# A 90-degree rotation on one core: all loads and stores on one SP queue in a fixed order, in place of loads on SP and stores on ACT

## The chip, the cores and the metric

The kernel runs on one core of one Trainium2 chip. The metric is device time in microseconds (us), the median of repeated executions. The profile's span, from the first to the last instruction, is about 1.8 us shorter than that time. With one core there is no second die to compare with.

## The reference

```python
def setup_inputs():
    batch, c, h, w = 32, 3, 256, 256
    return {"x": np.random.randn(batch, c, h, w).astype(np.float32)}

def reference(x):
    return np.rot90(x, k=-1, axes=(-2, -1)).astype(np.float32)
```

96 images of 256 x 256 fp32 are turned by 90 degrees. 25.17 MB are read and 25.17 MB written; there is no arithmetic.

## The kernel before

The images are cut into 24 slabs of 1 MB. Each of the 128 partitions holds 8 whole rows (8 KB, contiguous in memory on both sides). VectorE turns a slab with two transposes; it reads one tile and writes another, so loads, transposes and stores of different slabs can overlap.

```python
    in_pool = ctx.enter_context(tc.tile_pool(name="in_pool", bufs=12))
    out_pool = ctx.enter_context(tc.tile_pool(name="out_pool", bufs=12))

    for n in range(n_slabs):                                  # 24 slabs
        t_in = in_pool.tile([P, R * W], fp32, tag="t_in")
        nc.sync.dma_start(out=t_in, in_=ld_v[n])              # load: SP queue

        t_out = out_pool.tile([P, R * W], fp32, tag="t_out")
        src = t_in.rearrange("p (r g c) -> p c r g", r=R, c=R)
        dst = t_out.rearrange("p (c g r) -> p c r g", c=R, r=R)[:, :, ::-1, ::-1]
        for k in range(PARTS):                                # 2 transposes
            cs = slice(k * CP, (k + 1) * CP)
            nc.vector.transpose(out=dst[:, cs], in_=src[:, cs])

        nc.scalar.dma_start(out=st_v[n], in_=t_out)           # store: ACT queue
# ... (shapes, views and launch cut)
```

## Time and profile before

| | before |
|---|---|
| median time | 124.7 us |
| span of the profiled execution | 122.9 us |
| bytes moved | 50.34 MB |
| VectorE busy | 94.6 us (77%) |
| loads, stores: issue to landing, median | 19.6 us, 16.5 us |

First the page of the profile before. The rows with 40 figures cut the span into 40 equal slices of 3.07 us: busy tenths for an engine or for the 16 DMA engines (9 is 90% or more), then the rate in GB/s. q1 is the SP queue, q10 the ACT queue, q14 the one that the page calls instruction; the last column is the share of the 16 engines' time.

```profile
span 122.9 us, 186 instructions
...
DVE  0199999999897697796977967979769779797500
...
DMA  2999999999999999999999999999999999999994
GB/s 93 427 427 403 339 424 427 427 429 427 427 432 427 427 427 427 432 429 427 427 427 427 429 427 427 427 427 429 427 427 427 427 429 427 427 429 427 427 424 171
...
q1 hardware_dynamic: 3456, 25.17, 49.2%
q10 hardware_dynamic: 3456, 25.17, 48.5%
...
DMA 89%; DVE 2%; DVEq 2%; SPq 1%; issue 0%
```

The DMA engines are full in every slice but the first and last, the rate is near 427 GB/s, and 89% of the chain of waits is DMA. VectorE has gaps. This kernel is limited by data movement alone: 50.33 MB at 427 GB/s take 117.9 us of the span's 122.9. The rest is the start (the first packet starts at 1.80 us), the exit, and one dip. The dip is in slices 4 and 5 (403, 339), seen finer in the stretches of 1 us of before; the last two columns are the DMA share and GB/s:

```profile
10.00:11.00 1.00, 1.00 (x1) 0.00 (x0) 1.00 1.07 451
11.00:12.00 1.00, 1.00 (x2) 0.00 (x0) 1.00 0.94 360
12.00:13.00 1.00, 1.00 (x1) 0.00 (x0) 1.00 1.06 311
13.00:14.00 1.00, 1.00 (x2) 0.00 (x0) 1.00 0.96 287
14.00:15.00 1.00, 1.00 (x1) 0.00 (x0) 1.00 0.94 393
15.00:16.00 1.00, 1.00 (x2) 0.00 (x0) 1.00 0.99 418
```

Against 427, the four low rows lack 67 + 116 + 140 + 34 = 357 KB, which is 0.84 us at that rate, although the engines count as busy (share near 1). Here a DMA share near 1 stood beside 287 GB/s as well as beside 427, so read the share beside the rate. In the trace's packet records, the loads' 8 KB packets took 393 ns on average from 11 to 15 us, against 309 ns from 5 to 10 us. The first store had been issued at 9.67 us. The page also counts 768 packets under 512 B, 16 for each of the 48 transfers; in the packet records they have 4 bytes and took 9 ns each. The expectations below call them completion records.

One more view will matter: the way out, as the groups of the exit line of before (count; shortest, median and longest in ns; start of the first and of the last in us). SP's first DRAIN, at 122.16 us, comes after SP's last wait on a transfer, which ended at 122.12; POOL's semaphore steps run from 122.2 to 122.8 us, and the span ends at 122.9.

```profile
L79 POOLq EVENT_SEMAPHORE  x4: 17/17/17, 122.2 to 122.8; - x4
L79 SPq DRAIN  x3: 7/7/7, 122.2 to 122.5; - x3
```

### The profile page before, as it was taken

The numbers are of one execution on the slowest core, as the hardware profiler recorded it, in microseconds if no ns is written. First come the engines' busy times: TensorE is split into PE (matmuls) and PEld (weight loads), VectorE is DVE, ScalarE is ACT, GpSimd is POOL, SyncE is SP. The second block draws the span as 40 slices with busy tenths as digits, with TensorE's granted clock in tenths as the row PEclk, the third lists the DMA queues.
The fourth block names the chain that finished last, engine by engine and source line by source line (L and its number), as shares of the span: only waits on it lengthen the run. The fifth ranks groups of instructions, "written<-read, shape, count | busy, mean of one in ns | idle before, by whom it ended". The sixth has DMA issues, their size and how long they took to land.

```text
span 122.9 us, 186 instructions
## 1 busy us (share of the span) xinstructions
DVE 94.6 (77%) x48; POOL 0.2 (0%) x4
## 2 busy tenths in 40 slices
DVE  0199999999897697796977967979769779797500
POOL 0000000000000000000000000000000000000000
DMA  2999999999999999999999999999999999999994
GB/s 93 427 427 403 339 424 427 427 429 427 427 432 427 427 427 427 432 429 427 427 427 427 429 427 427 427 427 429 427 427 427 427 429 427 427 429 427 427 424 171
DMA packets 6913, 50.34 MB, mean 410 GB/s; under 512 B 768, under 2 KB 768, under 8 KB 768
## 3 DMA queue, kind: packets, MB, share of 16 engines
q1 hardware_dynamic: 3456, 25.17, 49.2%
q10 hardware_dynamic: 3456, 25.17, 48.5%
q14 instruction: 1, 0.01, 0.0%
HBM read 25.17 MB, written 25.17 MB: 410 GB/s over the span
## 4 chain that ended last, share of the span: by engine, by line
DMA 89%; DVE 2%; DVEq 2%; SPq 1%; issue 0%
DMA t_in<-in_x_dram 89%; DVE t_out L51 2%; DVEq L79 2%; SPq L44 1%; DVEq L51 0%
## 5 line engine op out<-in xcount | busy, mean ns | idle before, releaser
L51 DVE STREAM_TRANSPOSE t_out<-t_in 128x1024 f32<-128x1024 f32 x48 | 94.6, 2052 | 20.9 <-DMA t_in<-in_x_dram 15.4
L68 POOL MEMSET const-uint8-127<- 128x1 uint8 x1 | 0.1, 102 | 0.0
L68 POOL MEMSET const-bfloat16-1.0<- 128x1 bf16 x1 | 0.1, 101 | 0.0
L68 POOL MEMSET const-float32-0.0<- 128x1 f32 x1 | 0.1, 98 | 0.2 <-issue 0.2
L68 POOL MEMSET const-float32-1.0<- 128x1 f32 x1 | 0.1, 98 | 0.0
## 6 DMA issues: line engine op xcount, KB each, us to landing
t_in<-in_x_dram SPq DMA_DIRECT2D x24, 1024.0 KB, 19.6
out_dram<-t_out ACTq DMA_DIRECT2D x24, 1024.0 KB, 16.5
```

The costliest lines, as they stand in the source:

```text
L44: nc.sync.dma_start(out=t_in, in_=ld_v[n])
L51: nc.vector.transpose(out=dst[:, cs], in_=src[:, cs])
L68: nc = _bacc.Bacc("TRN2", target_bir_lowering=False, num_devices=1)
L79: with _tile.TileContext(nc) as tc:
```

## The change

The intent: let one queue carry all transfers in an order that the program fixes, so that loads stay a set distance of nine slabs ahead and each store takes its turn.

```diff
+    AHEAD = 9
+    ins = []
+
+    def load(n):
+        t_in = in_pool.tile([P, R * W], fp32, tag="t_in")
+        last = nc.sync.dma_start(out=t_in, in_=ld_v[n])
+        ins.append(t_in)
+        return last
+
+    for n in range(AHEAD):
+        load(n)
+
     for n in range(n_slabs):
-        t_in = in_pool.tile([P, R * W], fp32, tag="t_in")
-        nc.sync.dma_start(out=t_in, in_=ld_v[n])
         t_out = out_pool.tile([P, R * W], fp32, tag="t_out")
-        src = t_in.rearrange("p (r g c) -> p c r g", r=R, c=R)
+        src = ins[n].rearrange("p (r g c) -> p c r g", r=R, c=R)
         # ... transposes as before
-        nc.scalar.dma_start(out=st_v[n], in_=t_out)
+        nc.sync.dma_start(out=st_v[n], in_=t_out)
+        if n + AHEAD < n_slabs:
+            load(n + AHEAD)
```

Each transfer waits for the landing of the one eight places earlier in the order, because the compiled program has eight semaphores for transfers (99, 100 and 102 to 107 in both traces). Before, loads held four of the eight in steady state (99, 102, 104, 106) and stores the other four. If only the loop is rewritten, with stores left on ACT, the compiled order is the same as before (built and compared, not run): on two queues the rewritten loop is no change at all. The change therefore is the one queue. It takes SP from 24 transfers to 48.

## The prediction

> **What bounds the kernel now.** The 16 DMA engines. The page's slice rows show DMA at 9 (90% or more) in every slice but the first and last, with 427 GB/s in most. The kernel moves 50.33 MB; at 427 GB/s that is an estimated 117.9 us of the 122.9 us span. The stretch table shows where the other 5 us are: nothing moves before about 2 us; after 121.1 us there is only the last receipt and the exit (1.91 us at the end of the chain of waits); and from 11 to 15 us the rate is 360, 311, 287, 393 GB/s while the DMA engines stay busy, which lacks about 0.36 MB, or 0.84 us. This dip comes just as the first store, issued at 9.67 us, mixes with the loads. VectorE is no limit: two transposes take 3.98 us a slab, against 4.9 us for a load plus a store. [...]
>
> **What the change does.** It adds no bytes, transpose or transfer. 24 stores move from the ACT queue to SP, which then issues 48 transfers of about 0.33 us, one per 2.45 us of transfer: no limit. [...] the rate is 427 with loads alone (4 to 10 us), with both mixed, and with stores alone (after 112 us). A mixed single queue no trace shows yet.
>
> Will the fixed order starve the engines? In the compiled order each transfer waits for the one eight places before it, and each store for its transposes. Eight transfers are 19.6 us of work. Slab n's transposes end at about 9.5 + 3.9n us; its store's turn comes at about 2 + 2.45 x (9 + 2n) = 24 + 4.9n us. The slack is 14 us and grows. At the end nine stores go out in a row; the last load lands near 98 us, its transposes end near 103 us, and its store is not due before about 117 us. VectorE is not exposed at the tail.
>
> **On the critical path.** Only the 0.84 us dip can go, if the two queues cause it; if it is a cost of the first stores, it moves to about 24 us and stays. Half of it, 0.4 us, is my expected gain. Against it stands a risk: switching direction inside one queue may cost a gap. [...]
>
> **Predicted time: 124.3 us**, 8 in 10 between 123.3 and 126.2. Faster by over 2%: 0.04; within 2%: 0.87; slower by over 2%: 0.09.
>
> **What would show each step.** Right: one queue with near 98% of the engines' time, 427 GB/s from 3 to 120 us, no dip at 11 to 15 us; SP's waits all on transfers, never long on VectorE; VectorE's last work near 103 us, stores alone in the last 20 us; landing near 19.6 us for both kinds. Wrong: a mixed stretch (24 to 100 us) below 420 GB/s with DMA busy (a switching cost), or slices with DMA under 9 in the middle (starved: SP held by a wait).
>
> **What would make it wrong.** A queue too shallow for eight transfers, so that SP stalls; a switch cost; or a gain in the mixed stretch from runs in one direction, which loads alone, at 427, speak against.

## The result, and the profile after

| | before | after |
|---|---|---|
| median time | 124.72 us (124.66 to 124.83) | 125.12 us (125.09 to 125.14) |
| span of the profiled execution | 122.9 us | 123.3 us |
| VectorE's last transpose ends (timeline) | 115.4 us | 104.0 us |
| loads, stores: issue to landing, median | 19.6, 16.5 us | 19.6, 19.6 us |

The ratio is 1.0031, with a 95% interval of 1.0013 to 1.0048: the same within 2%, but a real 0.4 us slower. Ratios here are the mean time of one kernel's fast runs over that of the other's fast runs of the same rounds, so not quite the ratio of the medians. Executions over 1.5% slower than the fastest of the same kernel are left out of the means.

The page after:

```profile
span 123.3 us, 177 instructions
...
DVE  0199999999999999999999996796976977000000
...
DMA  3999999999999999999999999999999999999993
GB/s 93 422 428 428 425 425 422 353 388 428 428 425 428 425 428 428 428 425 428 428 425 428 428 425 430 433 425 425 428 428 428 425 428 428 428 422 428 430 425 130
...
q1 hardware_dynamic: 6912, 50.33, 97.7%
```

One queue now takes 97.7% of the engines' time, as both together did, and at the same rate. The stretch table gives 427 GB/s over 30 to 100 us in both kernels. VectorE works without gaps from 5.6 to 74.6 us, because loads are far ahead, and is done 19 us before the end; none of that made the run shorter (125.12 us against 124.72). The dip is in slices 8 and 9 now. After, by microsecond:

```profile
22.00:23.00 1.00, 1.00 (x2) 0.00 (x0) 1.00 1.05 434
23.00:24.00 1.00, 1.00 (x1) 0.00 (x0) 1.00 1.16 360
24.00:25.00 1.00, 1.00 (x2) 0.00 (x0) 1.00 1.04 246
25.00:26.00 1.00, 1.00 (x1) 0.00 (x0) 1.00 0.82 328
26.00:27.00 1.00, 1.00 (x2) 0.00 (x0) 1.00 0.98 418
```

It lacks 67 + 181 + 99 = 347 KB, or 0.81 us, against 0.84 before. It has moved to the time when the first store gets its turn behind nine loads (9 x 2.45 us after the first bytes), and has kept its size.

SP's own waits, after (what SP waited for; us in total, times, longest):

```profile
SPq L65 <- DMA out_dram<-t_out: 34.1, 16, 2.2
SPq L50 <- DMA t_in<-in_x_dram: 30.3, 16, 3.0
...
SPq L65 <- DVE t_out L63: 3.7, 4, 1.5
```

A store that waits for VectorE holds up every load behind it in the fixed order: ahead_2, below, waited so for 118.5 us and took 147.25 us. Here it happened four times, by 1.5 us at most, with up to 19.6 us of transfers queued ahead.

So where do the 0.4 us come from? Not from the transfers. The records of SP's last wait on a transfer start at 122.09 us before and 122.06 us after: by SP's waits, the changed kernel had all its data in place 0.04 us earlier. The difference comes after that. The exit line's groups, after:

```profile
L93 POOLq EVENT_SEMAPHORE  x4: 17/17/17, 122.7 to 123.2; - x4
...
L93 SPq DRAIN  x3: 7/7/130, 122.1 to 122.9; - x3
```

SP's first DRAIN comes at 122.1 (122.2 before), but POOL's answer to the second comes at 122.7 (122.2 before), and one DRAIN now takes 130 ns in place of 7. In the trace's records SP's first two DRAINs start at 122.160 and 122.215 before (0.06 us apart), and at 122.125 and 122.535 after (0.41 us apart). From SP's first DRAIN to POOL's answer it is 0.09 us before and 0.57 us after: 0.48 us more, less the 0.04 us gained, is the 0.44 us between the spans (122.89 and 123.33 in the records).

### The profile page after: what moved, and what is told of

It reads as the page before. It is cut to its first block, busy times and chain, and to the rows that moved or that the text cites. A ratio compares the mean times of both kernels' runs of the same rounds, so it can differ in the third digit from the quotient of the medians.

```text
span 123.3 us, 177 instructions
## 1 busy us (share of the span) xinstructions
DVE 92.9 (75%) x48; POOL 0.2 (0%) x4
## 3 DMA queue, kind: packets, MB, share of 16 engines
q1 hardware_dynamic: 6912, 50.33, 97.7%
## 4 chain that ended last, share of the span: by engine, by line
DMA 77%; SPq 2%; DVE 2%; DVEq 2%; issue 1%
DMA t_in<-in_x_dram 77%; SPq L50 2%; DVE t_out L63 2%; DVEq L93 2%
## 5 line engine op out<-in xcount | busy, mean ns | idle before, releaser
L63 DVE STREAM_TRANSPOSE t_out<-t_in 128x1024 f32<-128x1024 f32 x48 | 92.9, 2048 | 11.1 <-DMA t_in<-in_x_dram 5.6
## 6 DMA issues: line engine op xcount, KB each, us to landing
t_in<-in_x_dram SPq DMA_DIRECT2D x24, 1024.0 KB, 19.6
out_dram<-t_out SPq DMA_DIRECT2D x24, 1024.0 KB, 19.6
```

## The experiments

Two questions were open: what makes SP pause on its way out, and what the dip is. For the pause, theory A says that it belongs to the length of SP's instruction list; its rival B says that it belongs to the queue that issued the last stores. For the dip, theory F says that it comes once, with the first store; its rival M says that it comes with every turn from a stretch of loads to stores. All twelve kernels gave correct results. Diffs are against the changed kernel, unless it is said that they are against the one before.

### The last store back on ACT (last_store_act)

```diff
-        nc.sync.dma_start(out=st_v[n], in_=t_out)
+        q = nc.scalar if n == n_slabs - 1 else nc.sync
+        q.dma_start(out=st_v[n], in_=t_out)
```

> The changed kernel, with only the last of the 24 stores moved back to the ACT queue. The traces of before and after show the last store landed at the same time (SP's last wait ends 122.12 and 122.08 us), and then 0.55 us less or more on the way out: SP's second exit step follows its first by 0.06 us before, by 0.41 us after. Theory A (length): SP's instruction list is now twice as long[...]; one store less changes nothing, the gap stays near 0.4 us and the time near 125.1 us. Theory B (owner): the queue that issued the last store pays on its way out; with the last store on ACT the gap on SP goes to under 0.1 us and the time to about 124.7 us.

Measured: 124.96 us (124.87 to 124.98), ratio 1.0013 (1.0001 to 1.0025), between the two expectations. The exit groups tell why:

```profile
L94 POOLq EVENT_SEMAPHORE  x4: 17/17/17, 122.2 to 123.0; - x4
L94 SPq DRAIN  x3: 7/7/130, 122.1 to 122.7; - x3
```

The long DRAIN of 130 ns is still there, but POOL's first answer is back at 122.2: it is the third DRAIN now that comes late (122.745 us, 0.60 us after the second, against 0.24 us before). One transfer less takes two instructions out of SP's list (87 to 85), and the pause came two of SP's records later. Counted from the start of the trace, it is before SP's 80th record in both kernels. Part of it is now hidden: from SP's first DRAIN to the end of the span it is 1.00 us here, 1.21 in the changed kernel and 0.73 in the one before. This refutes the sharp form of B (the pause follows the last store) and suggests a fixed place in SP's list.

### Two slabs in one transfer (two_slabs)

```diff
-    AHEAD = 9
+    AHEAD = 4
+    S = 2                                   # tiles [P, S, R * W], 6 buffers each
-    ... .rearrange("(n p r) w -> n p (r w)", p=P, r=R)
+    ... .rearrange("(n s p r) w -> n p s (r w)", s=S, p=P, r=R)
 # ... stores likewise; transposes loop over s
```

> The changed kernel with two slabs (2 MB) in each transfer: one SP queue, four double loads ahead, 24 transfers in all in place of 48, all on SP. Theory A (length): SP has no more instructions than before, so the exit gap of 0.4 us is gone and the time is at most 124.7 us; with half the completion records (9 ns each, 24 fewer on each engine, 0.2 us) about 124.5 us. Theory B (owner): SP still issues the last store, the gap of 0.4 us stays, and the time is about 124.9 us. The dip at the first store should stay in both, near 23 us.

Measured: 125.28 to 127.15 us in the five fast executions (median 125.76), a wide scatter. The time misses both expectations. SP waited 12 times and 90.7 us in all for VectorE, since a double slab is ready only after four transposes, and the last data landed later (SP's first DRAIN at 122.7); that the waits caused this was not shown. The exit itself, with the last store on SP and a list of 49 instructions, has no pause: SP's DRAINs are 0.06 and 0.24 us apart, as before:

```profile
L95 SPq DRAIN  x3: 7/7/7, 122.7 to 123.0; - x3
```

That is A and not B. The dip was smaller here: 328 and 377 GB/s from 21 to 23 us lack 99 + 50 = 149 KB, or 0.35 us.

### Loads in halves of 64 partitions, stores on ACT (half_loads; against before)

```diff
-        nc.sync.dma_start(out=t_in, in_=ld_v[n])
+        for h in (slice(0, P // 2), slice(P // 2, P)):
+            nc.sync.dma_start(out=t_in[h], in_=ld_v[n][h])
```

> The kernel before with each load cut in two halves of 64 partitions: 48 loads on SP, 24 stores on ACT. SP's list is as long as in the changed kernel, but no store is on SP. Theory A (length): the exit gap on SP rises to about 0.4 us. Theory B (owner): it stays at 0.06 us. The time has 24 more completion records per engine, 9 ns each, 0.2 us: about 125.3 us under A, 124.9 us under B; the trace decides rather than the time.

Measured: 147.32 to 148.76 us in the three fast executions, wrong by about 23 us, and no pause. As a test of the pause it failed, because SP's list turned out to be 75 instructions (71 records) and not 87: it ends before the 80th record, so neither theory is touched. The time taught something else. Rates by slice, in half_loads:

```profile
DMA  5999999999999999999999999999999999999936
GB/s 115 215 215 215 213 374 363 416 379 379 226 292 385 401 385 326 365 279 397 403 423 281 379 399 385 401 383 365 405 392 350 401 383 379 421 321 370 419 159 250
```

While only half loads ran (slices 2 to 5) the rate was 215 GB/s, just half of 428, with the DMA engines busy all the time. The packet records say how: from 4 to 15 us an 8 KB packet took 605 ns on average, against 309 ns in the loads of before. Each packet took twice as long. The column cuts below ask whether the partitions or the size did it.

### A small store at the very start (warm_store)

```diff
+    warm_pool = ctx.enter_context(tc.tile_pool(name="warm_pool", bufs=1))
+    scratch = nc.dram_tensor("scratch", (P, 128), fp32, kind="Internal").ap()
+    t_w = warm_pool.tile([P, 128], fp32, tag="t_w")
+    nc.vector.memset(t_w, 0.0)
+    nc.scalar.dma_start(out=scratch, in_=t_w)
```

> The changed kernel with one extra store of 64 KB of zeros to a scratch tensor, on the ACT queue, issued at the very start. The dip (360, 246, 328 GB/s at 23 to 26 us in the changed kernel, 360, 311, 287, 393 at 11 to 15 us before) came with the first store in both. Theory F (first store, once per run): the dip moves to the first 5 us, none at 23 to 26 us; time between 124.3 (hidden in the start) and 125.2 us. Theory M (the turn from loads alone to a mix): the dip stays at 23 to 26 us, and the time stays at 125.1 us or 0.2 us more.

Measured: 125.12 us (125.11 to 125.28), as the changed kernel. The stretches around the dip:

```profile
23.00:24.00 1.00, 1.00 (x2) 0.00 (x0) 1.00 1.00 418
24.00:25.00 1.00, 1.00 (x2) 0.00 (x0) 1.00 1.08 336
25.00:26.00 1.00, 1.00 (x2) 0.00 (x0) 1.00 0.91 352
26.00:27.00 1.00, 1.00 (x2) 0.00 (x0) 1.00 0.97 410
```

The dip is still there, with half its size (91 + 75 + 17 = 183 KB, 0.43 us). The start was slower (106 GB/s from 2 to 3 us, 197 without the extra store), and nothing was won in total. Neither theory says "half": inconclusive. It does show that a small early store cannot buy the dip off.

### One store cut in two (split_store)

```diff
-        nc.sync.dma_start(out=st_v[n], in_=t_out)
+        cuts = (0, R * W // 2, R * W) if n == 12 else (0, R * W)
+        for lo, hi in zip(cuts, cuts[1:]):
+            nc.sync.dma_start(out=st_v[n][:, lo:hi], in_=t_out[:, lo:hi])
```

> The changed kernel with one store of the middle (slab 12) cut into two column halves: SP's list grows from 87 to 89 instructions, SP still issues the last store. So far the pause on SP's way out came before the same record in the changed kernel and with the last store moved (the 80th of SP's records, 0.41 and 0.60 us after the step before it, against 0.05 and 0.24 us where there is no pause), and not at all in lists of 75 or 49 instructions. Theory A, made sharper (a pause of about 0.36 us at a fixed place in SP's list, once): two more instructions push that place back into SP's wait for the last stores, where it is hidden; SP's exit steps are 0.05 and 0.24 us apart, and the time falls from 125.1 to about 124.8 us (0.1 us of it lost to 8 more packets per engine). Theory C (any list of this length pays on its way out): the pause stays at the exit and the time is 125.1 to 125.2 us.

Measured: 125.16 us (124.94 to 125.53). The exit is as theory A had it, with no long DRAIN:

```profile
L95 POOLq EVENT_SEMAPHORE  x4: 17/17/17, 123.1 to 123.6; - x4
L95 SPq DRAIN  x3: 7/7/7, 123.0 to 123.3; - x3
```

Two instructions more, and the pause is gone from the exit: SP's 80th record is now its last wait for a store (from 119.9 us), where theory A has the pause hidden. This rules out theory C, that any list of that length pays at the exit. But the median time did not fall: in the profile the last data arrived late, with SP's first DRAIN at 123.0 in place of 122.1 us. This profile is of the second slowest of six executions (125.49 us); the two fastest took 124.94 and 124.98 us. One thing in the records fits. In the six runs with the pause in the exit, an 8 KB packet of the instruction queue q14 started 0.63 to 0.92 us after SP's 80th record, after all data; here it ran at 121.6 us for 0.31 us, among the last packets of stores. Whether this made the last store late is not shown, and it would not account for all of the 0.9 us. The expected gain in time is a miss.

### The last two and the last four stores on ACT (last_two_act, last_four_act)

```diff
-        nc.sync.dma_start(out=st_v[n], in_=t_out)
+        q = nc.scalar if n >= n_slabs - 2 else nc.sync       # last_four_act: - 4
+        q.dma_start(out=st_v[n], in_=t_out)
```

> The changed kernel with the last two stores on ACT: SP's list is 83 instructions, so it should end just before the place of the pause. Theory A: no pause in the exit at all, time about 124.7 us. Theory C or a pause tied to the last stores: it stays, 125.0 us.

> The changed kernel with the last four stores on ACT; SP's list is 79 instructions, against 87 (125.1 us), 85 (125.0 us, pause in the last exit step) and 83 (124.5 us, no pause). Theory A (one pause at a fixed place in SP's list): a step, not a slope; the time is that of the list of 83, 124.4 to 124.7 us. Rival D (every store that leaves the SP queue saves time): some 0.3 us less again, about 124.2 us.

Measured: with two, 124.50 us (124.48 to 124.76), ratio 0.9986 (0.9974 to 0.9998); with four, 124.89 us (124.58 to 124.96), ratio 1.0012 (1.0000 to 1.0025). The exit of last_two_act:

```profile
L94 POOLq EVENT_SEMAPHORE  x4: 17/17/17, 122.3 to 122.9; - x4
...
L94 SPq DRAIN  x3: 7/7/7, 122.2 to 122.5; - x3
```

Both lists (83 and 79 instructions; 79 and 75 records) end before the 80th record, and neither exit has the pause. The spans are 123.0 and 122.9 us, against 122.9 before and 123.3 after. Rival D, a saving for each store moved, is out: four are not faster than two. The two medians differ by 0.4 us in the direction that no theory has, with scatter within each run of 0.3 to 0.4 us, so times this close were not told apart. The medians of the spans, 122.7 and 122.9 us, differ by half as much.

### Loads in column halves, stores on ACT (column_loads; against before)

```diff
-        nc.sync.dma_start(out=t_in, in_=ld_v[n])
+        pieces = 4 if n % 4 == 1 else 2
+        step = R * W // pieces
+        for lo in range(0, R * W, step):
+            nc.sync.dma_start(out=t_in[:, lo:lo + step], in_=ld_v[n][:, lo:lo + step])
```

> The kernel before, stores on ACT, each load cut into two column halves (4 KB rows), and every fourth slab into four, so that SP's list has 87 instructions as in the changed kernel, with no store on SP. Theory A: the pause of about 0.36 us comes on SP's way out, at the same record from the end as in the changed kernel (0.41 us between its first two exit steps in place of 0.06). Theory B (the queue that owns the stores pays): none. Second question, why loads in halves of 64 partitions ran at 215 GB/s (3 to 15 us): if it was the half-size transfer, loads alone run near 215 GB/s here too; if it was the 64 partitions, they run near 420. The time then is about 126.5 us: some 12 more packets per slab and engine at 8 ns, an estimate from 309 ns for 8 KB and 7 to 9 ns for packets of 4 to 24 B.

Here SP's list has 87 instructions, as in the changed kernel, with no store in it. The exit groups:

```profile
L82 POOLq EVENT_SEMAPHORE  x4: 17/17/17, 137.7 to 138.3; - x4
L82 SPq DRAIN  x3: 7/7/131, 137.1 to 137.9; - x3
```

The pause is there, before SP's 80th record again: its first two DRAINs start at 137.147 and 137.575 us, 0.43 us apart. With the stores on ACT, B is refuted, and A in its sharper form (a fixed place in the list) confirmed.

The time, 139.59 us, was expected near 126.5: a miss of 13 us. Eight smaller transfers in flight are less data in flight, but while loads alone ran this was not the limit: from 4 to 14 us the DMA share was 0.98 at 340 GB/s, and the packets were slow for their size (4 KB in 181 ns on average, 2 KB in 101; a half and a quarter of 309 would be 155 and 77). What else delayed the run is open. Rates by slice:

```profile
DMA  4899999999999999999999999999999999999663
GB/s 111 310 347 352 429 436 411 422 300 398 413 396 416 399 345 298 425 422 416 356 388 311 409 419 421 391 377 306 349 424 406 416 347 360 324 419 414 253 261 159
```

Against half_loads: pieces of 512 KB (some of 256 KB) over 128 partitions ran at 310 to 352 GB/s in slices 2 to 4, over 64 partitions at 215. So the smaller pieces cost part (their size or their rows of 4 and 2 KB in place of 8, not told apart), and the 64 partitions cost more. In half_loads the two halves of a slab followed each other in one queue; halves on two queues at once were not tried.

### Eight loads, eight stores, three times (groups_of_8)

```diff
-    for n in range(AHEAD):
-        load(n)
-    for n in range(n_slabs):   # ... transposes, store, load(n + AHEAD)
+    for g in range(0, n_slabs, GROUP):          # GROUP = 8
+        for n in range(g, g + GROUP):
+            load(n)
+        for n in range(g, g + GROUP):
+            turn(n)                             # the two transposes
+            nc.sync.dma_start(out=st_v[n], in_=outs[n])
```

> One SP queue in another fixed order: eight loads, eight stores, three times. No more switches than 5 in place of about 30. Theory F (the dip comes with the first store, once): one dip of about 0.8 us near 22 us, time 125.1 us. Theory M (each turn from a long stretch of loads to stores): dips near 22, 61 and 100 us, time about 126.7 us. A cost of each switch of direction, too small to be seen in the changed kernel, would make this kernel faster; 30 switches at 427 GB/s leave no room for over 0.2 us.

Measured: 127.22 us (126.58 to 127.92), slower than either theory had it for that reason alone. Stretches of groups_of_8:

```profile
20.00:21.00 1.00, 1.00 (x2) 0.00 (x0) 1.00 1.17 418
21.00:22.00 1.00, 1.00 (x2) 0.00 (x0) 1.00 0.88 254
22.00:23.00 1.00, 1.00 (x2) 0.00 (x0) 1.00 0.84 262
...
63.00:64.00 1.00, 1.00 (x1) 0.00 (x0) 1.00 1.03 434
64.00:65.00 1.00, 1.00 (x2) 0.00 (x0) 1.00 1.05 442
...
121.00:122.00 1.00, 0.00 (x0) 0.00 (x0) 1.00 0.64 270
122.00:123.00 1.00, 0.00 (x0) 0.00 (x0) 1.00 0.39 164
123.00:124.00 1.00, 0.00 (x0) 0.00 (x0) 1.00 0.10 41
```

The first turn from loads to stores lacks 173 + 165 = 338 KB, 0.79 us. The second, near 64 us, shows nothing; the third, at 101 us, lacks 67 KB (360 GB/s), 0.16 us. The turns back from stores to loads lack about 0.29 us (303 GB/s at 45 us) and 0.16 us (393 twice at 84 to 86 us). So the large dip comes once, with the first stores (F, in the main), and M is refuted in the size that it needed. The rest of the loss is at the end: SP waited 24 times and 83.4 us for VectorE, which could not start the last eight slabs before their loads came, and the rate fell to 270, 164 and 41 GB/s after 121 us. The expectation had left this out.

### The changed kernel again (after_again)

> The changed kernel itself, unaltered, on the same chip as the run with four stores moved: 125.0 to 125.2 us and 0.3% over before, with the pause of about 0.4 us before the 80th of SP's records. It tells whether the difference from before belongs to the kernel or to the chip.

Measured: 125.08 us (125.04 to 125.36), ratio 1.0035 (1.0023 to 1.0048), with SP's first two DRAINs 0.42 us apart and a span of 123.4 us. The difference belongs to the kernel, not to a chip.

### Two or three loads ahead in place of nine (ahead_2, ahead_3)

```diff
-    AHEAD = 9
+    AHEAD = 2                                # ahead_3: 3
```

> The changed kernel with 2 in place of 9 loads ahead: only two transfers, 4.9 us, stand between a load and its own store in the queue, and the store needs about 4.0 us of transposes, 0.3 us of issue[...]. If the order's slack is what keeps the engines busy (the prediction's reason), the queue runs dry by about 0.3 us a slab, SP waits on VectorE, DMA falls under 95% in the middle, and the time is about 133 us (128 to 140). If the queue alone did it, the time stays at 125.1 us.

> The changed kernel with 3 loads ahead: four transfers, 9.8 us, between a load and its store[...]. The middle should not starve (427 GB/s); the start loses about 1.3 us (three loads are done before the first store may go) and the tail about 0.6 us: about 127 us. Were the slack of 14 us needed in full, this would run near ahead_2.

Measured: 147.25 us (146.88 to 147.78) with two, 127.84 us (127.46 to 128.56) with three. In ahead_2, the page's rates and then SP's waits:

```profile
GB/s 139 427 362 259 319 373 409 295 376 425 328 340 414 355 349 394 371 328 355 394 353 373 337 328 418 385 306 389 398 331 351 331 423 353 315 418 378 331 142 148
...
SPq L65 <- DVE t_out L63: 118.5, 24, 7.6
```

Every one of the 24 stores held up SP, for 118.5 us in all, where in the changed kernel four did for 3.7 us. The edit is the number of loads ahead alone, so this shows what the nine are for: in a single ordered queue, a store that is not ready stops the loads behind it. The expectation had the cause but a loss that was too small, 8 us in place of 22; DMA shares of 0.94 to 1.00 through most of the middle hid it, as packets took longer (347 ns on average, 313 ns in the changed kernel); why they did is open. With three, the middle runs at 423 to 428 GB/s, and the losses are at the start (306 GB/s from 10 to 15 us) and at the tail (225 GB/s from 120 to 122 us), as expected, with 2.7 us in all in place of 1.9. Yet SP waited for VectorE 24 times in ahead_3 too, and long:

```profile
SPq L65 <- DVE t_out L63: 95.6, 24, 7.5
```

So a long wait of SP is not yet a loss. It becomes one when the transfers already issued no longer keep the rate near 427 GB/s (423 to 428 in the middle of ahead_3, 337 to 392 in that of ahead_2).

## Why the prediction was right

The measured 125.12 us lie in the range of 123.3 to 126.2 us, and the class "within 2%" is right. The reason given, that the DMA engines are full at 427 GB/s and one queue carries that rate as well as two, is what the profile shows. Point by point:

- **What bounds it.** Right: 427 GB/s over 30 to 100 us in both kernels, one queue at 97.7% of the engines' time, two at 49.2% and 48.5%. Whether more than 427 GB/s could be had was not shown.
- **Switching direction inside one queue.** The feared cost did not come: the mixed stretch is at 427. groups_of_8, with 5 turns in place of about 30, showed no gain from fewer turns.
- **The fixed order does not starve.** Right for nine loads ahead: four waits on VectorE, 1.5 us at most. ahead_2 and ahead_3 show that the slack was needed, and that three of the nine already nearly do.
- **VectorE done near 103 us, stores alone at the end, landing near 19.6 us for both.** Right: 104.0 us, and 19.6 us for both.
- **The dip of 0.84 us.** The prediction left two cases open and took half of the gain. The second held: the dip came with the first stores, moved to 23 to 26 us, and kept 0.81 us. The expected gain of 0.4 us should have been about zero. What the dip is made of stays open: a small early store halved it and gained nothing.
- **What was missing.** The prediction has no term for a longer exit. SP's longer list brought a pause that put 0.44 us on the span. A term of 0 for the dip and one of about +0.4 us for the exit would have given 125.1 us. So the point estimate had the wrong sign, 0.4 us faster where 0.4 us slower was measured; the range covered it because both errors are small beside the 117.9 us of transfers. The prediction also read the exit wrongly: its 1.91 us at the end of the chain is VectorE's own closing DRAIN (113.5 to 115.4 us), and the way out from SP's first DRAIN took 0.73 us before.

That the pause stands at a fixed place in SP's list is shown: it came before the 80th of SP's records in all six exits that reach that record with steps left to delay (the changed kernel twice, last_store_act, warm_store, column_loads, groups_of_8), and in none of the lists that end earlier (before, two_slabs, half_loads, last_two_act, last_four_act). In split_store it would fall into a wait, where it cannot be seen. In ahead_2 and ahead_3 the 80th record is the very last; it starts 0.44 and 0.45 us after the end of the one before, against 0.36 us for the last record of the kernel before and of the changed one, which fits a pause mostly hidden behind another wait.

What the pause is made of is not shown. One thing in the records lies near it: an 8 KB packet of the instruction queue started 0.6 to 0.9 us after the 80th record in all eight runs that reach it in the exit. But the packet starts when the pause is over (at 123.19 us in the changed kernel, where the 130 ns DRAIN ended at 122.67), so it is not what SP waited for. The traces do not say which engine such a packet serves, and last_two_act and last_four_act, without the pause, have one too, 1.3 and 1.8 us after the end of the span.

No kernel here clearly beats the one before. The best, last_two_act (one queue but for two stores, without the pause), has a ratio of 0.9986 (0.9974 to 0.9998), about 0.2 us. Its profiled execution (124.76 us, span 123.0) was the slowest of five; the other four had spans of 122.7 to 122.8 us, against 122.9 to 123.1 in the runs of before. It was not repeated, so equal to before is all that is safe to say.

## What to carry to other kernels

Here, where 427 GB/s held nearly from start to end, the choice of queue and the order of transfers were worth nothing by themselves. An order could lose, by making a ready load wait behind a store that is not ready (147.25 us with two loads ahead, 125.12 with nine); so measure its slack (transfers between a load and its store) against the compute time. Before explaining a difference of half a microsecond by the main loop, compare when the last transfer landed: here that was the same, and all of the difference was on the way out, in the instruction list of the queue that had taken over the work. A test of such a place is to make the list a few instructions longer or shorter and see whether the pause moves.
